# The small transposes move into the score banks: three PSUM banks plus one become four

## The chip, the cores and the metric

The kernel runs on one core of a Trainium2 chip. The metric is the device time of one execution in microseconds (us); less is better. Five engines take instructions in order, each from its own queue: TensorE (PE: matmuls and transposes; PEld is its weight load), VectorE (DVE), ScalarE (ACT), GpSimd (POOL) and SyncE (SP, which issues the DMAs).

## The reference, cut to what matters

One layer of a decoder trunk on a sequence of 2048 tokens, width 1024: an RMSNorm, one input projection, three causal attention branches (differential, forgetting, dilated), each times a SiLU gate and projected back, a sigmoid gate per channel, a sum, an output projection with residual, a last RMSNorm.

```python
h = rmsnorm(x, norm_g)
p = split(h @ w_in)                      # q, k, v, z of three branches, f, merge gates
ya = rmsnorm(diff_attention(qa, ka, va, lam, slopes)) * 0.8 * silu(za)      # 4 heads, two softmaxes each
yb = forgetting_attention(qb, kb, vb, cumsum(log_sigmoid(f + fb))) * silu(zb)  # 8 heads
yc = dilated_attention(qc, kc, vc, slopes) * silu(zc)                       # 8 heads, 3 dilations
merged = sum(sigmoid(gate_n) * (y_n @ w_branch[n]) for n in 3)
out = rmsnorm(x + merged @ w_out)
```

All of it is float32. The kernel gets near that from float16 matmuls: every operand is split into a high and a low float16 part, and a product takes three (or two) matmuls.

## The kernel before, in words

The work is cut into 12 groups, four to a branch (two heads of 64 columns each). A group has three kinds of work that are woven into each other:

- **Score work.** `softmax_rows` (L654, for the first two branches) makes, for 128 query rows, chunks of up to 512 keys. For a chunk it takes a PSUM bank with `sc_bank` (L274, pool `ps_sc`, three banks), `scores` (L641) writes two matmuls into it (L643 and L644), and one DVE operation (L678, two where the diagonal is in the chunk) adds the bias, writes the sum into an SBUF tile `e` and keeps the row maximum. With that read the bank is free. ACT then takes the exponential (L691), ACT and DVE split the tile into two float16 halves in place (L702, L703), a DMA transposes it (L712, into `eT`), which frees the `e` tile (there are five, `E_SLOTS`), and PE multiplies `eT` with the values (L695, L696) into a bank of `ps_po` (two banks). `jobs_dil` (L1007) does the same for the third branch with a bank for each block of 128 queries and two heads (DVE read at L1049, exponential at L1055).
- **Filler work.** Projections of this and the next group (`proj_unit`, `fill_v`, `fill_z`, `gate_unit`), 24 matmuls of 512 columns (L371, `mm_steps`) for each output bank of `ps_dn` (two banks).
- **Chains.** Weights are loaded a unit ahead and prepared: the largest absolute value (`abs_max`, L283), a power of two from it (`global_pow2`, L201), two splits (`w_split`, L298). `global_pow2` needs the maximum over all 128 partitions: it transposes a column on PE into a PSUM bank (L204), and DVE reduces it (L206, tile `E_...`). Before, that bank `pb_...` came from a pool of its own, `ps_tr`, with one bank. The same bank took the two prefix sums of the forgetting gates (L892 to L908, once in the kernel, by `tr_bank`, L268) and the transposed norm weights at the start (L1459). `global_pow2` is called for each weight unit, for each group's gated output (`post`, L1135), for the branch weights (`prep_b2`, L1287) and the output weights (`prep_out`, L1390): 98 calls.

So PSUM's eight banks are divided 1 (`ps_tr`) + 2 (`ps_dn`) + 3 (`ps_sc`) + 2 (`ps_po`).

Four stages follow each other in time. In the first 100 us x is normalised and transposed (`x_phase`, L623, which takes 32 turns in `ps_sc`). Then come the differential groups (to about 880 us), the forgetting groups (to about 1665 us) and the dilated groups (to about 2360 us), and last a tail with the branch projections (`branch`, L1309) and the output projection (`out_mm`, L1407). The tail takes its banks in turn from `ps_po`, `ps_sc` and `ps_dn` (`tail_bank`, L1305); the bank of `ps_tr` has no part in that.

The order of the work: `drive` (L1178) interleaves score jobs, value products and, by planned costs (`Filler.pump`, L134), filler steps and chain steps; this gives the order in which the program is written down. Beyond that the context is opened with `schedule_with_timeline_sim=True` (L1606): at build time the library takes the written order as priority, and puts each engine's instructions into an order of its own, by when, in its planned timeline, operands and a buffer of the pool are there. What engine does what when is then fixed; on the chip each engine keeps that order and waits on semaphores. The number of banks in a pool is an input to that order.

Of the kernel before, what the change touches and what calls it, by code (L numbers as in the profile page):

```python
# [11 lines left out]
F32 = mybir.dt.float32  # L12
# [4 lines left out]
PSUM = bass.MemoryType.PSUM  # L17
DRAM = bass.MemoryType.DRAM

P = 128  # L20
# [133 lines left out]
def tile_hybrid_trunk(  # L154
# [20 lines left out]
    cp = ctx.enter_context(tc.tile_pool(name="cp", bufs=1))  # L175
    st = ctx.enter_context(tc.tile_pool(name="st", bufs=4))
    dr = ctx.enter_context(tc.tile_pool(name="dr", bufs=1, space=DRAM))
    ps_tr = ctx.enter_context(tc.tile_pool(name="ps_tr", bufs=1, space=PSUM))
    ps_dn = ctx.enter_context(tc.tile_pool(name="ps_dn", bufs=2, space=PSUM))

    ident = cp.tile([P, P], F32, name="ident")
# [7 lines left out]
    def hp(n):  # L189
        return tc.high_priority(offset=n) if n else nullcontext()  # L190

    def pow2_floor(dst, src):
        V.tensor_single_scalar(dst.bitcast(I32), src.bitcast(I32), EXPMASK, op=ALU.bitwise_and)
# [5 lines left out]
        pow2_floor(dst, dst)  # L199

    def global_pow2(col, name):  # L201
        pb = ps_tr.tile([P, 512], F32, tag="tr", name=f"pb_{name}")
        with hp(H_PB):
            T.transpose(pb[:, :P], col.to_broadcast([P, P]), ident)  # L204
        E = st.tile([P, 1], F32, tag="gp", name=f"E_{name}")
        V.tensor_reduce(E, pb[:, :P], axis=AX.X, op=ALU.max)  # L206
        V.tensor_scalar(E, E, 1e-30, None, op0=ALU.max)
        pow2_floor(E, E)
        return E
# [16 lines left out]

    mn = ExitStack()
    big = mn.enter_context(tc.tile_pool(name="big", bufs=1))
    ps_sc = mn.enter_context(tc.tile_pool(name="ps_sc", bufs=3, space=PSUM))
    ps_po = mn.enter_context(tc.tile_pool(name="ps_po", bufs=2, space=PSUM))  # L230

    def e_tile(name, shape=(P, 1024), dt=F32):
# [31 lines left out]

    def gs_tile(name):
        return big.tile([P, 512], F32, tag="gs", name=name, bufs=GS)

    def tr_bank(name):  # L268
        return ps_tr.tile([P, 512], F32, tag="tr", name=name)

    def dn_bank(name):
        return ps_dn.tile([P, 512], F32, tag="dn", name=name)
# [1 line left out]
    def sc_bank(name):  # L274
        return ps_sc.tile([P, 512], F32, tag="sc", name=name)
# [41 lines left out]
    def w_scale(am, name):  # L317
        E = global_pow2(am, name)
        sw = st1("sw", f"sw_{name}", 1, 2)
        pow2_over(sw, E, 13)  # L320
        dsc = st1("dsc", f"dsc_{name}", 1, 2)
        V.tensor_scalar(dsc, E, ixs, 2.0 ** -13, op0=ALU.mult, op1=ALU.mult)
        return sw, dsc
# [509 lines left out]
    def prep_f():  # L833
        ft = bl_tile("fw")
        stg = ft[:, 0:64].rearrange("p (k c) -> p k c", c=8)
        Q.dma_start(stg, w2[:, OFF_FF:OFF_FF + 8].rearrange("(k p) c -> p k c", p=P))
        fb = st1("fb", "fb", 8, 1)
        Q.dma_start(fb, fox_fb.to_broadcast([P, 8]))
        yield 4000
        am = st1("amf", "am_f", 1, 1)  # L840
        V.tensor_reduce(am, stg, axis=AX.XY, op=ALU.max, apply_absolute_value=True)
        yield 2000
        E = global_pow2(am, "f")
        sw = st1("swf", "sw_f", 1, 1)
        pow2_over(sw, E, 13)
        wt = ft[:, 64:128].bitcast(F16).rearrange("p (a k c) -> p a k c", a=2, c=8)
        A.activation(wt[:, 0], stg, AF.Copy, scale=sw)
        V.scalar_tensor_tensor(wt[:, 1], stg, sw, wt[:, 0], op0=ALU.mult, op1=ALU.subtract)
        dsc = st1("dscf", "dsc_f", 1, 1)
        V.tensor_scalar(dsc, E, ixs, 2.0 ** -13, op0=ALU.mult, op1=ALU.mult)  # L850
        fbox.update(fb=fb, wt=wt, dsc=dsc)

    def fill_f():
# [12 lines left out]
        f = ft[:, 0:128]  # L866
# [22 lines left out]
        G.memset(one, 1.0)  # L889
        G.affine_select(out=tri, in_=one, pattern=[[1, P]], compare_op=ALU.is_ge, fill=0.0, base=0, channel_multiplier=-1)  # L890
        yield 4000
        pc = tr_bank("pcum")  # L892
        T.matmul(pc[:, 0:128], tri, f, start=True, stop=True)
        T.matmul(pc[:, 128:256], one, f, start=True, stop=True)
        tot_ = ft[:, 896:1024]
# [6 lines left out]
            V.tensor_add(tot[:, b], tot[:, b], tot[:, b - 1])  # L902
        V.tensor_add(cs[:, 1:NB], cs[:, 1:NB], tot[:, 0:NB - 1])
        yield 5000
        pt = tr_bank("pcs")
        T.transpose(pt[:, :P], cs_, ident)
        csT = ft[:, 128:256]
        A.activation(csT, pt[:, :P], AF.Copy)  # L908
# [226 lines left out]
    def post(gr):  # L1135
# [13 lines left out]
        am = yield from abs_max(z, "u" + n)  # L1149
        yield YU  # L1150
        E = global_pow2(am, "u" + n)
        s = st1("us", f"us_{n}", 1, 2)
        pow2_over(s, E, 13)
# [302 lines left out]
    xb0 = x_load(0)  # L1456
    gx = cp.tile([P, KC], F32, name="gx")
    ixs = cp.tile([P, 1], F32, name="ixs")
    pb = ps_tr.tile([P, 512], F32, tag="tr", name="pb_g")  # L1459
    T.transpose(pb[:, :KC], g8, ident[:KC, :KC])  # L1460
    V.tensor_copy(gx, pb[:, :KC])
    gm = st.tile([P, 1], F32, tag="gm", name="gm")
# [147 lines left out]
```

## Time and profile before

| | us |
|---|---|
| three timed runs | 2789.35 (median), 2782.40, 2799.62 |
| the profiled execution: first to last instruction (span) | 2783.2 |
| PE busy in it | 2624.6 (94%) |
| DVE busy | 2088.2 (75%) |
| ACT busy | 1661.3 (60%) |
| POOL busy | 376.8 (14%) |
| mean granted PE clock | 0.985 |

The profiled execution's own device time isn't given beside its span; its span lies 6.15 us under the median of the timed runs and inside their spread. "Busy" is the union of instruction times; a PE matmul's record overlaps the next one's. "Idle before" an instruction is the time in which its engine had nothing running, and the name behind the arrow is what released it. The granted clock is 1.00 at 2.4 GHz and 0.50 at 1.2 GHz.

### The profile page before, as it was taken

How to read it: one execution, taken by the hardware profiler on the slowest of the kernel's cores; microseconds unless marked ns; L12 is line 12 of the kernel's file. 1: busy time of each engine (PE TensorE's matmuls, PEld its weight loads, DVE VectorE, ACT ScalarE, POOL GpSimd, SP SyncE). 2: the span in 40 equal slices, each digit the busy share in tenths (PEclk: the TensorE clock that was granted, in tenths of full speed). 3: DMA queues.
4: the chain of work that ended last, by engine and by line, in shares of the span. 5: the costliest groups of instructions: out<-in, count | busy, mean ns of one | idle time of the engine just before them, and what ended most of it. 6: DMA issues, size and time to landing. Idle time of an engine off the chain costs nothing.

```text
span 2783.2 us, 47508 instructions
## 1 busy us (share of the span) xinstructions
PE 2624.6 (94%) x16216; PEld 1376.9 (49%) x16216; DVE 2088.2 (75%) x7048; ACT 1661.3 (60%) x3616; POOL 376.8 (14%) x529
## 2 busy tenths in 40 slices
PE   7999899999999999999899999999999999999998
PEld 4454445455444454444444444554554545444565
DVE  8687877978877878768778776658568575778955
ACT  6466666656556676666666665656657678535411
POOL 0000200200201112002102110005033051210000
PEclk9999999989999999999999999999999999999999
DMA  4345444445454786787787777648568599875232
GB/s 160 76 84 114 74 100 107 104 76 123 87 100 106 135 173 142 155 154 157 144 155 145 141 144 156 132 108 180 126 132 185 125 210 230 226 210 163 80 121 76
DMA packets 979268, 376.94 MB, mean 135 GB/s; under 512 B 834120, under 2 KB 939344, under 8 KB 977488
## 3 DMA queue, kind: packets, MB, share of 16 engines
q1 hardware_dynamic: 979024, 373.90, 61.9%
q8 instruction: 127, 2.08, 0.3%
q14 instruction: 117, 0.96, 0.1%
HBM read 118.14 MB, written 59.05 MB: 64 GB/s over the span
## 4 chain that ended last, share of the span: by engine, by line
PE 52%; DVE 19%; DMA 17%; ACT 7%; issue 4%; POOL 1%; SPq 1%; DVEq 0%; ACTq 0%; POOLq 0%
DMA eT_g<-e_g 11%; PE pg L371 10%; PE pbr L371 8%; PE pq_g L371 8%; PE pz_g L371 5%; PE pout L1417 4%; PE s_g L643 4%; DVE e_g L678 4%; PE s_g L644 4%; DVE e_g L703 4%; PE po_g L695 3%; ACT e_g L691 3%; PE pv_g L371 2%; PE pout L1418 2%; DMA w_g<-in_w_in_dram 2%
## 5 line engine op out<-in xcount | busy, mean ns | idle before, releaser
L371 PE MATMUL pg<-xT,w_g 128*128 128x512 f16 x2304 | 554.5, 382 | 0.3 <-ACT xT L638 0.3
L691 ACT ACTIVATE e_g<-e_g,nm_g,c_g 128x1024 f32<-128x1024 f32 (+7 forms) x384 | 377.6, 984 | 263.5 <-DVE nm_g L685 227.9
L643 PE MATMUL s_g<-stk_g 128*128 128x512 f16 (+3 forms) x1024 | 352.6, 352 | 50.2 <-DVE pm_g L678 45.6
L703 DVE SCALAR_TENSOR_TENSOR e_g<-e_g 128x512 f16<-128x512 f32 (+2 forms) x480 | 316.0, 670 | 80.9 <-ACT e_g L702 79.6
L371 PE MATMUL pq_g<-xT,w_q 128*128 128x512 f16 x1536 | 369.5, 387 | 5.0 <-DVE stk_g L398 4.4
L695 PE MATMUL po_g<-v_g,eT_g 128*128 128x128 f16 (+1 forms) x2232 | 306.7, 235 | 61.5 <-DMA eT_g<-e_g 56.2
L644 PE MATMUL s_g<-stk_g,q_g 128*128 128x512 f16 (+3 forms) x1024 | 351.9, 354 | 2.6 <-DMA q_g<-stk_g 2.6
L371 PEld LDWEIGHTS <-w_g 128*128 128x128 f16 x2304 | 218.9, 99 | 229.9 <-issue 5.3
L702 ACT ACTIVATE e_g<-e_g 128x512 f16<-128x512 f32 (+2 forms) x480 | 265.0, 569 | 104.4 <-DVE e_g L703 102.3
L696 PE MATMUL po_g<-v_g,eT_g 128*128 128x64 f16 (+1 forms) x2232 | 286.3, 201 | 0.0
L695 PEld LDWEIGHTS <-eT_g 128*128 128x128 f16 x2232 | 207.2, 99 | 141.7 <-DMA eT_g<-e_g 88.4
L371 PE MATMUL pz_g<-xT,w_z 128*128 128x512 f16 x1152 | 273.1, 380 | 2.5 <-DVE stk_g L398 2.4
L371 PE MATMUL pv_g<-xT,w_v 128*128 128x512 f16 x1152 | 270.3, 382 | 4.3 <-DVE vs_g L527 4.3
L1055 ACT ACTIVATE e_g<-e_g,nm_g,c_g 128x256 f32<-128x256 f32 (+1 forms) x384 | 207.8, 543 | 91.4 <-DVE nm_g L1051 90.3
L371 PE MATMUL pbr<-u,w_b 128*128 128x512 f16 x1152 | 253.5, 381 | 0.0
L678 DVE CUSTOM_DVE_ANT_0 e_g<-s_g,bias_g 128x512 f32<-128x512 f32 (+3 forms) x320 | 187.8, 605 | 59.7 <-DMA eT_g<-e_g 51.6
L696 PEld LDWEIGHTS <-eT_g 128*128 128x128 f16 x2232 | 204.5, 99 | 49.5 <-issue 5.5
L371 PEld LDWEIGHTS <-w_q 128*128 128x128 f16 x1536 | 146.5, 100 | 166.4 <-issue 13.4
L678 DVE CUSTOM_DVE_ANT_0 e_g<-s_g,R_g 128x512 f32<-128x512 f32 (+3 forms) x288 | 171.2, 596 | 62.9 <-DMA eT_g<-e_g 55.4
L1049 DVE CUSTOM_DVE_ANT_0 e_g<-s_g,bd_g 128x256 f32<-128x256 f32 (+1 forms) x384 | 122.8, 361 | 89.0 <-PE s_g L644 44.7
L371 PEld LDWEIGHTS <-w_b 128*128 128x128 f16 x1152 | 112.9, 98 | 133.5 <-issue 2.2
L644 PEld LDWEIGHTS <-q_g 128*128 128x128 f16 x1024 | 109.2, 107 | 140.6 <-issue 62.3
(471 smaller groups left out, 4174.3 us busy)
## 6 DMA issues: line engine op xcount, KB each, us to landing
gd<-gs SPq DMA_DIRECT2D x96, 256.0 KB, 2.7
gt<-gd SPq DMA_DIRECT2D x24, 1024.0 KB, 5.3
w_g<-in_w_in_dram SPq DMA_DIRECT2D x24, 512.0 KB, 4.4
ud<-y_g SPq DMA_DIRECT2D x48, 256.0 KB, 2.8
od_g<-ro_g SPq DMA_DIRECT2D x64, 132.0 KB, 1.9
xb<-in_x_dram SPq DMA_DIRECT2D x16, 512.0 KB, 5.8
q_g<-stk_g SPq DMA_DIRECT2D x128, 64.0 KB, 2.2
w_q<-in_w_in_dram SPq DMA_DIRECT2D x32, 256.0 KB, 4.1
```

What stands on the lines that cost most here:

```text
L371: T.matmul(dst, l, r, start=(i == 0), stop=(i == n - 1))
L643: T.matmul(ps, stk[:, 0, qsl], stk[:, 1, ksl], start=True, stop=False)
L644: T.matmul(ps, q2s, stk[:, 1, ksl], start=False, stop=True)
L678: V.tensor_tensor_reduce(out=et[ch // 2][:, o + a:o + a + sw], in0=ps[:, a:a + sw], in1=b, scale=1.0, scalar=-3e38, op0=ALU.add, op1=ALU.m ...
L691: A.activation(e[:, 256:256 + w], e[:, 256:256 + w], AF.Exp, bias=nm, scale=gr["c"][u], accum_out=den_of(i))
L695: T.matmul(po, eh, vv, start=first, stop=False)
L696: T.matmul(po[:, 0], el, vv[:, 0], start=False, stop=last)
L702: A.activation(h[:, :w], f, AF.Copy, scale=scale)
L703: V.scalar_tensor_tensor(h[:, w:], f, scale, h[:, :w], op0=ALU.mult, op1=ALU.subtract)
L1049: V.tensor_tensor_reduce(out=e[:, o + w * u:o + w * u + w], in0=ps[:, 256 * u:256 * u + w], in1=bt[p, u][:, 256 - w:256], scale=1.0, scala ...
L1055: A.activation(eu, eu, AF.Exp, bias=nm[:, 2 * a + u:2 * a + u + 1], scale=gr["c"][u], accum_out=sm[:, a, 2 + u:3 + u])
L1417: T.matmul(po, ah, wo[un][k], start=k == 0, stop=False)
```

## The change

The pool `ps_tr` and the helper `tr_bank` go, `ps_sc` has four banks instead of three, and the four places that took `ps_tr`'s bank take the next bank of `ps_sc`. PSUM is then divided 2 + 4 + 2. Nothing else is changed: no instruction is added, removed or resized.

```diff
@@ -175,7 +175,6 @@
     cp = ctx.enter_context(tc.tile_pool(name="cp", bufs=1))
     st = ctx.enter_context(tc.tile_pool(name="st", bufs=4))
     dr = ctx.enter_context(tc.tile_pool(name="dr", bufs=1, space=DRAM))
-    ps_tr = ctx.enter_context(tc.tile_pool(name="ps_tr", bufs=1, space=PSUM))
     ps_dn = ctx.enter_context(tc.tile_pool(name="ps_dn", bufs=2, space=PSUM))
 
     ident = cp.tile([P, P], F32, name="ident")
@@ -199,7 +198,7 @@
         pow2_floor(dst, dst)
 
     def global_pow2(col, name):
-        pb = ps_tr.tile([P, 512], F32, tag="tr", name=f"pb_{name}")
+        pb = sc_bank(f"pb_{name}")
         with hp(H_PB):
             T.transpose(pb[:, :P], col.to_broadcast([P, P]), ident)
         E = st.tile([P, 1], F32, tag="gp", name=f"E_{name}")
@@ -226,7 +225,7 @@
 
     mn = ExitStack()
     big = mn.enter_context(tc.tile_pool(name="big", bufs=1))
-    ps_sc = mn.enter_context(tc.tile_pool(name="ps_sc", bufs=3, space=PSUM))
+    ps_sc = mn.enter_context(tc.tile_pool(name="ps_sc", bufs=4, space=PSUM))
     ps_po = mn.enter_context(tc.tile_pool(name="ps_po", bufs=2, space=PSUM))
 
     def e_tile(name, shape=(P, 1024), dt=F32):
@@ -264,9 +263,6 @@
 
     def gs_tile(name):
         return big.tile([P, 512], F32, tag="gs", name=name, bufs=GS)
-
-    def tr_bank(name):
-        return ps_tr.tile([P, 512], F32, tag="tr", name=name)
 
     def dn_bank(name):
         return ps_dn.tile([P, 512], F32, tag="dn", name=name)
@@ -889,7 +885,7 @@
         G.memset(one, 1.0)
         G.affine_select(out=tri, in_=one, pattern=[[1, P]], compare_op=ALU.is_ge, fill=0.0, base=0, channel_multiplier=-1)
         yield 4000
-        pc = tr_bank("pcum")
+        pc = sc_bank("pcum")
         T.matmul(pc[:, 0:128], tri, f, start=True, stop=True)
         T.matmul(pc[:, 128:256], one, f, start=True, stop=True)
         tot_ = ft[:, 896:1024]
@@ -902,7 +898,7 @@
             V.tensor_add(tot[:, b], tot[:, b], tot[:, b - 1])
         V.tensor_add(cs[:, 1:NB], cs[:, 1:NB], tot[:, 0:NB - 1])
         yield 5000
-        pt = tr_bank("pcs")
+        pt = sc_bank("pcs")
         T.transpose(pt[:, :P], cs_, ident)
         csT = ft[:, 128:256]
         A.activation(csT, pt[:, :P], AF.Copy)
@@ -1456,7 +1452,7 @@
     xb0 = x_load(0)
     gx = cp.tile([P, KC], F32, name="gx")
     ixs = cp.tile([P, 1], F32, name="ixs")
-    pb = ps_tr.tile([P, 512], F32, tag="tr", name="pb_g")
+    pb = sc_bank("pb_g")
     T.transpose(pb[:, :KC], g8, ident[:KC, :KC])
     V.tensor_copy(gx, pb[:, :KC])
     gm = st.tile([P, 1], F32, tag="gm", name="gm")
```

## Rows read from the trace of the kernel before

**Rows 1.** The page's first part: busy us, share of the span, instructions of PE.

```profile
PE 2624.6 (94%) x16216; PEld 1376.9 (49%) x16216; DVE 2088.2 (75%) x7048; ACT 1661.3 (60%) x3616; POOL 376.8 (14%) x529
```

**Rows 2.** Busy time by stage: stretch, its length, then each engine, clock, DMA.

```profile
0.00:100.00 100.00, 84.63 (x432) 46.89 (x433) 70.57 (x257) 58.40 (x112) 4.80 (x11) 1.00 0.41 127
...
100.00:880.00 780.00, 734.28 (x4389) 379.78 (x4388) 629.26 (x2054) 475.84 (x950) 68.99 (x61) 0.98 0.47 98
880.00:1665.00 785.00, 725.50 (x5116) 378.70 (x5114) 608.83 (x2132) 516.36 (x1053) 118.44 (x186) 1.00 0.77 148
1665.00:2360.00 695.00, 668.63 (x4075) 358.08 (x4076) 469.48 (x1761) 459.23 (x1226) 151.34 (x220) 0.97 0.74 158
2360.00:2783.20 423.20, 411.60 (x2209) 213.43 (x2207) 310.01 (x848) 151.50 (x279) 33.27 (x52) 0.99 0.49 146
```

**Rows 3.** PE's waits over the span: total us, times, longest.

```profile
PE po_g L695 <- DMA eT_g<-e_g: 56.2, 55, 3.1
PE s_g L643 <- DVE pm_g L678: 45.6, 64, 3.9
...
PE s_g L643 <- DVE s_g L1049: 3.7, 6, 1.1
```

**Rows 4.** Waits in the differential stage, 100 to 880 us.

```profile
DVE e_g L678 <- DMA eT_g<-e_g: 51.6, 31, 3.9
...
PE s_g L643 <- DVE pm_g L678: 33.8, 48, 3.9
```

**Rows 5.** Waits in the forgetting stage, 880 to 1665 us.

```profile
DVE e_g L678 <- DMA eT_g<-e_g: 71.8, 44, 4.8
...
PE po_g L695 <- DMA eT_g<-e_g: 39.1, 34, 2.4
...
PE s_g L643 <- DVE pm_g L678: 11.8, 16, 1.5
```

**Rows 6.** PE in order of time around 593 us: start, us, instruction, [idle before].

```profile
588.84 0.35 PE L371 MATMUL pf<-fw,xT 128*128 128x8 f16 x8
593.11 0.58 PE L643 MATMUL s_g<-stk_g 128*128 128x512 f16 x1 [3.91 <-DVE pm_g L678]
```

**Rows 7.** DVE in order of time before 593 us.

```profile
589.38 0.77 DVE L777 TENSOR_TENSOR den_g<-den_g 128x2 f32<-128x2 f32 x1 [2.31 <-ACT e_g L691]
...
590.63 1.81 DVE L784 SCALAR_TENSOR_TENSOR e_g<-e_g,a_g,e_g 128x1024 f32<-128x1024 f32 x2
592.36 0.68 DVE L678 CUSTOM_DVE_ANT_0 e_g<-s_g,bias_g 128x512 f32<-128x512 f32 x1
...
592.97 0.68 DVE L678 CUSTOM_DVE_ANT_0 e_g<-s_g,bias_g 128x512 f32<-128x512 f32 x1
```

**Rows 8.** All first score matmuls: count, ns min/median/max, first and last start.

```profile
L643 PE MATMUL s_g<-stk_g x1024: 216/379/634, 87.8 to 2361.9; 128*128 128x512 f16 x91, 128*128 128x256 f16 x38, 128*128 128x128 f16 x36, 128*128 128x384 f16 x6
```

**Rows 9.** PE in order of time around 1621 us.

```profile
1621.38 0.38 PE L371 MATMUL pg<-xT,w_g 128*128 128x512 f16 x1
...
1621.93 1.24 PE L371 MATMUL pg<-xT,w_g 128*128 128x512 f16 x5
```

**Rows 10.** Three stretches at the lower clock (the column behind POOL is PEclk).

```profile
103.58:113.82 10.24, 6.28 (x16) 2.00 (x16) 9.83 (x46) 5.59 (x12) 0.00 (x0) 0.50 0.38 73
339.10:342.51 3.41, 3.41 (x11) 1.32 (x9) 3.32 (x15) 3.37 (x6) 0.00 (x0) 0.50 0.46 86
584.86:601.92 17.06, 13.15 (x201) 8.89 (x199) 10.41 (x28) 12.27 (x19) 1.15 (x1) 0.50 0.49 87
```

**Rows 11.** Small transposes of L204: one group, and what PE idled for.

```profile
L204 PE MATMUL pb_ug<-ident,am_ug x12: 270/273/323, 328.7 to 2451.3; 128*128 128x128 f32 x12
...
  DVE am_g L292: 8.3, 4
```

**Rows 12.** The DVE reads (L206) of those transposes.

```profile
L206 DVE TENSOR_REDUCE E_ug<-pb_ug x12: 268/284/289, 337.1 to 2454.2; 128x1 f32<-128x128 f32 x12
```

**Rows 13.** DVE's waits over the span: dilated reads for their scores.

```profile
DVE e_g L1049 <- PE s_g L644: 44.7, 49, 3.1
```

## Prediction

> **What bounds the kernel now.** I read four views in this order: the page's busy shares, the busy time by stage, PE's waits, and then the trace in order of time around the longest of them.
>
> PE is busy for 2624.6 of 2783.2 us [rows 1], so 158.6 us is all that a better order of work can win, as long as no matmul goes away; none does. By stage [rows 2] PE idles 15.4 us in the first 100 us, 45.7 in the differential stage, 59.5 in the forgetting stage, 26.4 in the dilated stage and 11.6 in the tail. The other engines have room in every stage: DVE, the next, works 629.3 of 780 us in the differential stage, 81%.
>
> What does PE wait for [rows 3]? Two causes stand out: 56.2 us before value products, for the transposing DMA into eT, and 45.6 us before score matmuls, for the DVE read that frees a score bank, with 3.7 us more of this kind in the dilated stage. So waits for score banks cost 45.6 + 3.7 = 49.3 us, and this is what the change aims at. They sit in the differential stage above all: 33.8 us there, against 11.8 in the forgetting stage, where the wait for eT is larger with 39.1 [rows 4, 5].
>
> The longest bank wait shows how they come about [rows 6, 7]. PE's last matmul before it starts at 588.84, and the next score starts at 593.11, after 3.91 us idle. DVE meanwhile waited 2.31 us for an exponential, did the sums of a row and two combining operations (1.81 us), and only then, at 592.36, read the chunk whose bank PE needed; the next chunk's read followed at 592.97. DVE was late, with three finished chunks in front of it. A fourth bank would have let PE go on at 589.2.
>
> I paired the first 640 score chunks (the first two stages; the first and last of all score matmuls are at 87.8 and 2361.9 us [rows 8]) with their DVE reads in order. A chunk holds its bank for 4.8 us in the median; all three banks are held for 639 us; 122 chunks start within 0.15 us of the end of the read three chunks back, that is, as soon as a bank is free. Against the read four chunks back none starts sooner than 0.49 us after it. So in the order that PE has now, a fourth bank would end every one of these waits.
>
> **The change part by part.** *The fourth bank, order unchanged.* All 49.3 us of PE's idle time go. This is the upper end.
>
> *The fourth bank, order remade.* The order is not the written one: filler comes in steps of six matmuls, and around 1621 us such a step is cut into one and five with value products between them [rows 9]. The order is planned from what is free when, and with four banks it puts scores earlier until four are full in the plan. Where DVE runs behind the plan, PE then waits at the fourth bank as it now does at the third. The lower end is therefore 0, or below nothing where more scores are pulled forward than DVE follows with. The row nearest to the cost is the wait total itself; I take half of it, because DVE's lateness (2 to 4 us in the example) is about as large as what one more chunk adds (one read of 0.68 us plus the 3 us or so between chunks). Term: -25 us, bounds -49 to +10.
>
> *The clock.* Three stretches of 10.24, 3.41 and 17.06 us are granted 0.50, that is 1.2 GHz [rows 10]; in or right before each I find one of the longer bank waits (the one of 3.91 us lies in the third [rows 6]). Half of their 30.7 us, 15 us, is lost. In the third many matmuls of 8 columns run as well (those of the forgetting gates), so not all of it is the wait's doing. Term: -4 us, bounds -15 to 0.
>
> *What is late next.* PE that doesn't wait for a bank comes sooner to the value products, whose eT depends on DVE, ACT and a DMA and comes no sooner. DVE itself waits 51.6 and 71.8 us for eT in the first two attention stages, because all five e tiles are in use [rows 4, 5]; a bank doesn't change that. In the differential stage, where most of the gain lies, PE loses little to eT, in the forgetting stage much. I let a third of the 25 us come back: +8 us, bounds 0 to +25.
>
> *The transposes in the pool.* 98 transposes keep their time on PE. Each now holds a score bank from its start to its DVE read: in the group shown, 328.7 to 337.4 us for the first and 2451.3 to 2454.5 for the last [rows 11, 12]. Over the 98 pairs I find 2.9 us in the median, 8.7 at most, 316 us in all, 11% of the span. So scores have four banks nine tenths of the time, and three, as now, in the rest: no loss from the count. But a transpose now has to find a bank among the scores, and what waits behind it is a weight's scale, its two splits and then a projection. Weights are loaded a unit ahead, which covers some us. PE now idles 8.3 us in four cases before transposes of the gate weights [rows 11], because the maximum is late; that is the price of a late one, 2.1 us each. I take one or two such cases: +3 us, bounds -5 (a transpose no longer waits for the read of the one before) to +50 (the third rival).
>
> *Stages where I cost it at nothing.* In the first 100 us the 32 turns of x through the score banks get a fourth bank; PE idles 15.4 us there at most [rows 2], and mostly before operands, not banks: 0, bounds -3 to +2. In the dilated stage DVE waits 44.7 us for scores [rows 13], which a score placed earlier would shorten, but PE is busy for 96% there and is the one that sets the pace: 0, bounds -8 to +5. In the tail PE is busy for 411.6 of 423.2 us [rows 2]: 0, bounds -3 to +5. The two prefix sums are six short matmuls, once: 0.
>
> Sum: -25 - 4 + 8 + 3 = -18 us. Against the profiled execution's span of 2783.2 us that is 2765. The span lies 6.15 us below the median of the timed runs, and I add this back: 2771 us.
>
> **The rivals.** *First, the whole wait goes.* All 49.3 us end, half of the 15 us of clock comes back, nothing is returned, the transposes cost 3: -54, so 2735 us. For it: in the present order no chunk would wait, and the bank waits are mostly in the stage that loses little to eT. Against it: the order is remade.
>
> *Second, the wait changes its name.* The score loop (read, exponential, split, DMA, e tile) sets the pace, PE arrives earlier and stands before eT or before the fourth bank instead. Gain 0 to 5, transposes 3: 2783 to 2791, say 2788. For it: DVE waits 123 us for eT in two stages [rows 4, 5]. Against it: DVE is at work during the waits I looked at, and has 150 us of idle time in the differential stage. That the fourth bank isn't used belongs here too; that all three banks are held for 639 us speaks against this. [...]
>
> *Third, slower.* The small transposes lose the bank that only they used. One that is placed on PE before a bank is free, or whose maximum is late, holds up everything behind it on PE, and its late scale delays the splits and the next projection. At 2.1 us each [rows 11], 24 of the 98 cost 50 us, which eats up the 21 us of the other terms and 28 more; from there this decides. At 30 the loss is 63 - 21 = 42 us: 2831 us. Against it: the chains are run ahead of need, and a bank turns over in about 5 us.
>
> **How the numbers follow.** Forecast 0.44 (its own range 2754 to 2787), first rival 0.24, second 0.20, third 0.12. A measurement here can tell about 1% from no change, that is 28 us: faster means below 2761, slower above 2817. Faster is the first rival and the low edge of the forecast (0.07): 0.31. Slower is the third rival: 0.12. Same: 0.57. The range goes from 2728, a little below the first rival, to 2812, which leaves out the third rival and a small part of the first.
>
> **What would show it right or wrong.** Right: PE's wait before L643 for DVE falls from 45.6 us to about 25; its wait for eT grows from 56 to about 64; the stretch at 1.2 GHz around 104 or 339 us is gone; the time between a transpose of L204 and its read stays near 2.9 us. The first rival would show under 10 us before L643 and no growth before eT; the second, PE's idle time of 105 us in the first two attention stages unchanged under other names; the third, PE's idle time before L204 or before L371 (for weights) several times what it is now. The forecast is wrong if PE's idle time falls by less than 5 or more than 45 us.

## The result and the profile after

The changed kernel is slower: 2862.04 us in the median of four runs (2855.62 to 2865.36) against 2790.14 us (2782.40 to 2799.62) for the kernel before. The ratio is 1.0253, with a 95% interval of 1.0228 to 1.0278: 72 us more where I forecast 18 less, and above the 2812 us at which my range ended.

The profiled execution has a span of 2861.9 us, 78.7 more than before. Its page begins like this (PE, DVE, ACT and POOL as in [rows 1]; line numbers from the middle of the kernel on are 4 lower than before):

```profile
span 2861.9 us, 47473 instructions
...
PE 2651.6 (93%) x16216; PEld 1382.1 (48%) x16216; DVE 2088.0 (73%) x7048; ACT 1661.1 (58%) x3617; POOL 376.0 (13%) x529
```

DVE, ACT and POOL work as long as before. PE issues the same 16216 matmuls, but is busy 27.0 us longer and idle 2861.9 - 2651.6 = 210.3 us instead of 158.6, that is 51.7 us longer; 27.0 + 51.7 = 78.7 us, the whole difference. Most of the longer busy time is clock: summed over the trace, PE had 1.2 GHz granted for 127.0 us in 29 stretches, before for 87.5 us in 17. In these stretches it was at work for 112.2 us, before for 70.3, and half of the 41.9 us more, 21 us, is lost by this estimate.

PE's waits (columns as in [rows 3]) show where the idle time is:

```profile
PE po_g L691 <- DMA eT_g<-e_g: 89.8, 78, 3.4
PE s_g L639 <- DVE pm_g L674: 25.4, 41, 3.8
PE pq_g L367 <- DVE stk_g L394: 15.9, 11, 3.8
```

The wait for a score bank fell from 45.6 to 25.4 us, as forecast. The wait for eT rose by far more than that, from 56.2 to 89.8 us. PE's waits before projections (all names together, summed over the trace) rose from 14.1 to 36.9 us. Of these 13.8 and 31.2 us are waits for a bank of `ps_dn`: the projection needs the bank whose last result DVE or ACT still has to read into `stk_g`, `vs_g` or `gs`. The rest after, 5.7 us, is mostly for a weight's scale or split.

DVE's waits for eT, that is for a free `e` tile, were 51.6 us in the differential stage and 71.8 in the forgetting stage [rows 4, 5]. In the same two stages of the changed kernel (100 to 908 us, 908 to 1722 us) they are

```profile
DVE e_g L674 <- DMA eT_g<-e_g: 88.3, 37, 5.0
...
DVE e_g L674 <- DMA eT_g<-e_g: 97.4, 64, 5.2
```

So the score work now comes more unevenly: it fills the five `e` tiles and stands. That PE then has less filler left when it needs eT is my reading; no row shows it.

Cut at the first score of each stage, the stages answer to those of [rows 2] (same columns):

```profile
103.50:908.60 805.10, 741.96 (x4387) 380.82 (x4386) 626.30 (x2030) 466.48 (x936) 73.27 (x61) 0.97 0.45 92
908.60:1722.00 813.40, 737.43 (x5127) 382.34 (x5124) 620.47 (x2165) 524.42 (x1064) 113.53 (x185) 0.99 0.75 145
1722.00:2428.00 706.00, 674.33 (x4102) 359.85 (x4101) 462.18 (x1744) 457.87 (x1211) 150.63 (x221) 0.97 0.74 156
2428.00:2861.00 433.00, 412.28 (x2187) 211.95 (x2185) 311.28 (x866) 154.68 (x300) 33.82 (x52) 0.98 0.49 143
```

The kernel before, cut the same way, takes 791.2, 779.4, 703.6 and 421.0 us. The first score starts 15.6 us later than before, but the third group only 0.4 us later, so that start costs nothing. From there the loss grows: 14.0 us at the fourth group, 29.6 at the first forgetting group, 63.5 at the first dilated group, 66.3 at the last score, 78.7 at the end. It is made in the two stages that alternate scores with much else, and in the tail; the dilated stage adds 2.4.

**Where it happens in the trace.** The clearest place is the first prefix sum. PE in order of time, changed kernel:

```profile
613.38 0.59 PE L639 MATMUL s_g<-stk_g 128*128 128x512 f16 x1
...
614.19 0.63 PE L639 MATMUL s_g<-stk_g 128*128 128x512 f16 x1
...
615.68 6.09 PE L367 MATMUL pg<-xT,w_g 128*128 128x512 f16 x24
...
622.93 1.67 PE L367 MATMUL pg<-xT,w_g 128*128 128x512 f16 x7
...
624.94 13.76 PE L367 MATMUL pg<-xT,w_g 128*128 128x512 f16 x63
638.53 0.38 PE L889 MATMUL pcum<-ft 128*128 128x128 f32 x2
638.75 0.39 PE L890 MATMUL pcum<-ft 128*128 128x128 f32 x2
638.98 0.38 PE L639 MATMUL s_g<-stk_g 128*128 128x512 f16 x1
...
639.41 0.38 PE L639 MATMUL s_g<-stk_g 128*128 128x512 f16 x1
...
639.84 0.38 PE L639 MATMUL s_g<-stk_g 128*128 128x512 f16 x1
```

For 638.98 - 614.19 = 24.8 us no score is started. PE isn't idle: it runs 24 + 7 + 63 = 94 projection matmuls and some value products. Then the prefix sum comes, and right behind it three scores at once. The kernel before has this in the same place:

```profile
608.71 5.99 PE L371 MATMUL pg<-xT,w_g 128*128 128x512 f16 x27
614.54 0.22 PE L643 MATMUL s_g<-stk_g 128*128 128x128 f16 x1
...
614.65 0.38 PE L643 MATMUL s_g<-stk_g 128*128 128x512 f16 x1
...
615.95 3.40 PE L371 MATMUL pg<-xT,w_g 128*128 128x512 f16 x15
619.18 0.38 PE L643 MATMUL s_g<-stk_g 128*128 128x512 f16 x1
...
620.70 0.38 PE L893 MATMUL pcum<-ft 128*128 128x128 f32 x2
...
621.30 0.22 PE L643 MATMUL s_g<-stk_g 128*128 128x128 f16 x1
```

Scores go on until 1.5 us before the prefix sum. DVE in the changed kernel tells what the scores were behind:

```profile
621.83 0.68 DVE L674 CUSTOM_DVE_ANT_0 e_g<-s_g,bias_g 128x512 f32<-128x512 f32 x1
...
633.87 0.29 DVE L882 TENSOR_TENSOR ft<-ft 128x128 f32<-128x128 f32 x1
...
639.18 0.29 DVE L892 COPY ft<-pcum 128x128 f32<-128x128 f32 x1 [5.01 <-PE pcum L890]
...
639.66 0.68 DVE L674 CUSTOM_DVE_ANT_0 e_g<-s_g,bias_g 128x512 f32<-128x512 f32 x1
```

The prefix sum's operand `f` is ready at 634.2 us, after the long chain that computes the gates. DVE read the last score that it had at 621.83 us, and every bank was free from 622.5 on. The scores waited for no bank. They stood behind a prefix sum that stood behind its operand, and when it was there, PE still had the rest of 63 planned projection matmuls in front.

**The written order.** What holds the scores back is the library's build step. I compared, in the built programs, the order in which PE first writes the tiles of a pool with the order in which the kernel's text takes them (832 score tiles, 101 of small transposes and prefix sums):

```
tiles first written out of the written order   before   after
scores among themselves                          0        0
transposes and prefix sums among themselves      0        0
both kinds together, of 933                     73        0
```

Tiles of one pool are begun in the order in which they are written down. With two pools, 73 tiles are begun after one that is written later: 20 transposes or prefix sums that scores overtook, and 53 scores that a transpose overtook. With one pool, none. From this I infer (the planner itself leaves no trace): a transpose whose maximum isn't there yet stops the planning of every score written after it, the plan puts filler in the gap, and the scores follow in a burst. By that theory, D in the expectations below, the pool's common order is the cause and the bank count matters little. The order binds the other way too: a transpose can no longer overtake scores, so its scale can come late.

### The profile page after: what moved, and what is told of

Same layout as the page of the kernel before. It is cut to its first block, busy times and chain, and to the rows that moved or that the text cites. A ratio compares the mean times of both kernels' runs of the same rounds, so it can differ in the third digit from the quotient of the medians.

```text
span 2861.9 us, 47473 instructions
## 1 busy us (share of the span) xinstructions
PE 2651.6 (93%) x16216; PEld 1382.1 (48%) x16216; DVE 2088.0 (73%) x7048; ACT 1661.1 (58%) x3617; POOL 376.0 (13%) x529
## 4 chain that ended last, share of the span: by engine, by line
PE 43%; DMA 17%; DVE 15%; ACT 4%; issue 3%; SPq 1%; POOL 0%; DVEq 0%; ACTq 0%; POOLq 0%
DMA eT_g<-e_g 12%; PE pg L367 9%; PE pq_g L367 6%; PE pbr L367 5%; PE pz_g L367 4%; PE pout L1413 4%; PE s_g L639 4%; PE s_g L640 3%; DVE e_g L699 3%; DVE e_g L674 3%; PE po_g L691 2%; PE pv_g L367 2%; PE pout L1414 2%; DMA w_g<-in_w_in_dram 1%; ACT e_g L687 1%
## 5 line engine op out<-in xcount | busy, mean ns | idle before, releaser
L367 PE MATMUL pg<-xT,w_g 128*128 128x512 f16 x2304 | 545.9, 384 | 0.3 <-ACT w_g L298 0.3
L691 PE MATMUL po_g<-v_g,eT_g 128*128 128x128 f16 (+1 forms) x2232 | 299.1, 236 | 100.4 <-DMA eT_g<-e_g 89.8
L639 PE MATMUL s_g<-stk_g 128*128 128x512 f16 (+3 forms) x1024 | 354.0, 355 | 28.9 <-DVE pm_g L674 25.4
L367 PE MATMUL pv_g<-xT,w_v 128*128 128x512 f16 x1152 | 270.2, 383 | 12.4 <-DVE vs_g L523 5.2
L692 PE MATMUL po_g<-v_g,eT_g 128*128 128x64 f16 (+1 forms) x2232 | 280.5, 202 | 0.0
L367 PE MATMUL pbr<-u,w_b 128*128 128x512 f16 x1152 | 260.4, 388 | 6.8 <-DVE ro_g L1080 4.1
L692 PEld LDWEIGHTS <-eT_g 128*128 128x128 f16 x2232 | 204.4, 99 | 46.4 <-issue 13.8
L367 PEld LDWEIGHTS <-w_v 128*128 128x128 f16 x1152 | 111.5, 99 | 137.9 <-issue 15.4
```

The costliest lines, as they stand in the source:

```text
L367: T.matmul(dst, l, r, start=(i == 0), stop=(i == n - 1))
L639: T.matmul(ps, stk[:, 0, qsl], stk[:, 1, ksl], start=True, stop=False)
L691: T.matmul(po, eh, vv, start=first, stop=False)
L692: T.matmul(po[:, 0], el, vv[:, 0], start=False, stop=last)
```

## The experiments

All ratios are to the kernel before, run on the same chip; intervals are 95%. The kernel before had medians from 2785.2 to 2792.0 us in these groups.

**Sharing apart from the fourth bank.** `share3` is the changed kernel with three banks in `ps_sc`, so one bank of PSUM is unused:

```diff
-    ps_sc = mn.enter_context(tc.tile_pool(name="ps_sc", bufs=4, space=PSUM))
+    ps_sc = mn.enter_context(tc.tile_pool(name="ps_sc", bufs=3, space=PSUM))
```

> The small transposes and prefix sums share the score pool, but the pool keeps three banks (seven of eight banks used). Theory A, the fourth score bank lets the build place scores earlier and PE then stands before eT: little change, 2785 to 2810 us, PE's wait for eT near 56 us. Theory B, the sharing is what costs, late weight scales: most of the loss is here, 2835 to 2870 us. Theory C, any replanned order scatters the time by tens of us: anything from 2760 to 2860 us, without a pattern in the waits.

Measured: 2865.43 us, ratio 1.0271 (1.0243 to 1.0300). Its PE waits:

```profile
PE po_g L691 <- DMA eT_g<-e_g: 85.5, 67, 5.9
PE s_g L639 <- DVE pm_g L674: 44.3, 63, 2.3
PE pq_g L367 <- DVE stk_g L394: 12.6, 5, 5.1
```

That is theory B's range. The whole loss is there with three banks: +75 us. The fourth bank then takes 19 us off the wait for banks (44.3 to 25.4), but only 3 us off the time; the stages in the next section show where the rest goes.

`four_dn` gives the scores their four banks alone and puts the transposes and prefix sums in the two banks of the projections:

```diff
-        pb = sc_bank(f"pb_{name}")
+        pb = dn_bank(f"pb_{name}")
...
-        pc = sc_bank("pcum")
+        pc = dn_bank("pcum")
...
-        pt = sc_bank("pcs")
+        pt = dn_bank("pcs")
...
-    pb = sc_bank("pb_g")
+    pb = dn_bank("pb_g")
```

> Four score banks, and the small transposes and prefix sums share the two banks of the projections instead. Theory A: as slow as the changed kernel, 2845 to 2880 us, scores held in PSUM for about 6.5 us in the median as there, PE's wait for eT near 90 us. Theory B: at most as slow as before, 2750 to 2800 us, since no transpose waits behind scores. Theory C: anything from 2760 to 2880 us.

Measured: 2896.85 us, 1.0386 (1.0363 to 1.0409). Worse still, and above every range that I had expected. Here 66 of the 933 score and transpose tiles are out of written order, nearly as before, but of the 390 tiles of projections, transposes and prefix sums none is (before: 30). The price is paid by whatever shares the pool, so it isn't peculiar to the score banks. With a pool of two banks more than the order may be at work.

`oneoff` is the kernel before with only the two prefix sums moved, two tiles out of 101; the transposes keep their bank:

```diff
-        pc = tr_bank("pcum")
+        pc = sc_bank("pcum")
...
-        pt = tr_bank("pcs")
+        pt = sc_bank("pcs")
```

> Only the two prefix sum tiles, used once at about 620 us, move to the score pool; it keeps three banks and the transposes keep their own. Theories A and B: the time of before within 8 us (2782 to 2798). Theory C: the order after 620 us is planned anew, so the time differs from before by more than 15 us one way or the other.

Measured: 2813.44 us, 1.0091 (1.0064 to 1.0117), 23 us above the kernel before in the same group and outside the range of theories A and B. PE in order of time:

```profile
600.52 0.63 PE L643 MATMUL s_g<-stk_g 128*128 128x512 f16 x1
...
601.65 3.19 PE L371 MATMUL pg<-xT,w_g 128*128 128x512 f16 x14
...
605.99 1.03 PE L371 MATMUL pg<-xT,w_g 128*128 128x512 f16 x4
...
607.35 11.60 PE L371 MATMUL pg<-xT,w_g 128*128 128x512 f16 x53
618.79 0.38 PE L893 MATMUL pcum<-ft 128*128 128x128 f32 x2
...
619.23 0.38 PE L643 MATMUL s_g<-stk_g 128*128 128x512 f16 x1
```

The same gap without scores, 18.7 us here, comes with these two tiles alone.

**A fourth bank from another base.** The kernel before can't be given a fourth score bank with all else kept, as that makes nine. `po1_sc3` takes one of the value products' two banks away, and `po1_sc4` gives it to the scores; transposes stay apart in both:

```diff
-    ps_po = mn.enter_context(tc.tile_pool(name="ps_po", bufs=2, space=PSUM))
+    ps_po = mn.enter_context(tc.tile_pool(name="ps_po", bufs=1, space=PSUM))
```

> One bank instead of two for the value products, three score banks, the transposes have their own: the base for the next run. Between 2800 and 2900 us; no theory says more.

> As the run before it, with a fourth score bank and the transposes still apart. Theory A: 20 to 70 us slower than it. Theory D: not slower than it by more than 10 us, up to 40 us faster. Theory C: within 50 us either way.

Measured: 2948.02 us, 1.0573 (1.0540 to 1.0607), and 2965.30 us, 1.0632 (1.0609 to 1.0654). The base is slower than I had expected. From it the fourth bank costs 17 us, more than the 10 that theory D allows and less than the 20 that theory A asks for: PE's wait for score banks falls from 78.7 to 63.3 us, its waits for eT and behind `stk_g` rise from 44.1 to 53.3 and from 20.8 to 28.9. No gain from a fourth bank shows here, but 17 us is little more than another order makes by chance (below), and the base is another kernel.

**When the late steps are written.** `after_late2` raises planned costs in the chains, so that transposes and prefix sums are written down later, behind more scores; `before_late2` makes the same edit in the kernel before:

```diff
-YA = 3000
+YA = 9000
...
-        yield 2000
+        yield 8000
...
-        yield 4000
+        yield 10000
...
-        yield 5000
+        yield 11000
```

> The changed kernel, but the chains wait longer before they write a small transpose or prefix sum (planned 9000 instead of 3000 before the weight scales, 8000, 10000 and 11000 instead of 2000, 4000 and 5000 for the forgetting gates; the group outputs' scales as they were). Theory D, tiles of one pool are taken in the written order, so scores stand behind a transpose whose maximum isn't there yet: written later the transpose finds its operand ready, and half of the loss or more goes, 2785 to 2825 us. Theory A, the fourth bank makes scores come in bursts: still 2840 to 2880 us. Theory C, each new order scatters the time: anything from 2780 to 2880 us.

> The kernel before with the same later transposes, as the control: there they have their own bank, so theories A and D expect 2780 to 2805 us; theory C anything from 2780 to 2860 us.

Measured: 2841.00 us, 1.0172 (1.0153 to 1.0192), and 2815.21 us, 1.0083 (1.0064 to 1.0101). The edit wins 21 us in the changed kernel and costs 23 in the one before. Both miss theory D's ranges: it expected half of the loss or more to go, and the control to stay under 2805. The first lies just inside theory A's range. In the shared pool the wait for eT falls from 89.8 to 68.6 us. So the place in the text may matter to the shared pool, in the direction of theory D, but tuning it doesn't bring the loss back.

**How much any other order costs.** An order found anew may differ by chance. `jit1` and `jit2` change a planned cost slightly in the kernel before (YD from 3000 to 3050, and XF from 1.1 to 1.101); `after_jit1` and `after_jit2` do this in the changed kernel:

```diff
-YD = 3000
+YD = 3050
```

> The kernel before with one planned cost of the weight chains set from 3000 to 3050, which means nothing by itself but gives another order. Theories A and D: within 10 us of before. Theory C: 15 to 60 us away from it, and then likely slower.

> The kernel before with the planned filler stretched by 0.1% (XF 1.101 instead of 1.1), again nothing but another order. Theories A and D: within 10 us of before. Theory C: 15 to 60 us away from it, and then likely slower.

> The changed kernel with the planned cost of the weight chains at 3050 instead of 3000: another order, nothing else. If the loss of 72 us belongs to the change: 2840 to 2885 us. If it is the accident of one order: anything from 2780 to 2880, and likely under 2840.

> The changed kernel with the planned filler stretched by 0.1%: another order, nothing else. If the loss of 72 us belongs to the change: 2840 to 2885 us. If it is the accident of one order: anything from 2780 to 2880, and likely under 2840.

Measured: 1.0053 (1.0034 to 1.0072) and 1.0018 (1.0005 to 1.0030) for the kernel before, 2805.42 and 2795.56 us; 1.0271 (1.0238 to 1.0303) and 1.0263 (1.0233 to 1.0294) for the changed one, 2866.16 and 2864.83 us. The 13 us of `jit1` are more than the 10 that theories A and D allowed. Order by chance is worth up to half a per cent in these two tries, not two and a half, and the changed kernel keeps its loss in three orders. The loss belongs to the change. By the same measure `oneoff` is 0.4 to 0.7% above these two, with an interval that overlaps that of `jit1`, and `before_late2` little above `jit1`.

**The order alone.** `coupled` leaves the pools of the kernel before as they are, four pools and three score banks, and only makes PE begin score tiles, turns of x, transposes and prefix sums in their written order, by a dependency that orders the issue without a wait on the chip:

```diff
+    turn = [None]
+
+    def in_turn(ins):
+        if turn[0] is not None:
+            tc.add_manual_dep(ins.ins, turn[0].name, mybir.DependencyInfo(mybir.DependencyClass.NoSync, mybir.DependencyReason.DATA), reason="in_turn")
+        turn[0] = ins.ins
...
-            T.transpose(pb[:, :P], col.to_broadcast([P, P]), ident)
+            in_turn(T.transpose(pb[:, :P], col.to_broadcast([P, P]), ident))
```

and so for the first matmul of each other tile of the kinds named. `coupled_ug` orders only the scores, the turns of x and the 12 transposes for the groups' output scales (`pb_u...`); `coupled_rest` orders all but these 12.

> The kernel before with its own four pools and banks, but PE has to start the small transposes, prefix sums, transposes of x and scores in the order in which they are written (an order of issue, no wait for a result). Theory D, the loss of the change is this order, which a shared pool imposes: 2840 to 2880 us, though not one bank is shared. Theory A or a loss from the shared bank itself: within 20 us of before, 2780 to 2810. Theory C, any other order: 2790 to 2815, as the runs with slightly changed planned costs.

> As the run before it, but only the 12 transposes for the scale of a group's output are bound to the scores' order. Theory D with these as the ones written long before their operand is there: 2815 to 2850 us, half of the loss or more from an eighth of the transposes. If the transposes for the weights carry the loss: under 2812 us.

> The complement: all but those 12 are bound to the scores' order. Theory D with the 12 as the main cause: 2795 to 2825 us. If the transposes for the weights and the prefix sums carry the loss: 2830 to 2870 us.

Measured: `coupled` 2835.92 us, 1.0160 (1.0143 to 1.0177); `coupled_ug` 2808.78 us, 1.0065 (1.0050 to 1.0080); `coupled_rest` 2831.98 us, 1.0149 (1.0128 to 1.0170). No tile is moved, and about 45 us are lost: 4 us less than the low end of theory D's range, and well above those of A and C. `coupled_ug` and `coupled_rest` both came out as expected if the transposes for the weights and the prefix sums carry the loss. PE in `coupled`, at one of the 12 transposes:

```profile
749.82 0.38 PE L652 MATMUL s_g<-stk_g 128*128 128x512 f16 x1
...
752.64 4.05 PE L378 MATMUL pq_g<-xT,w_q 128*128 128x512 f16 x18
758.30 0.28 PE L706 MATMUL po_g<-v_g,eT_g 128*128 128x256 f16 x1 [1.61 <-DMA eT_g<-e_g]
...
759.60 0.28 PE L211 MATMUL pb_ug<-ident,am_ug 128*128 128x128 f32 x1
759.72 0.33 PE L652 MATMUL s_g<-stk_g 128*128 128x384 f16 x1
...
760.04 0.38 PE L652 MATMUL s_g<-stk_g 128*128 128x512 f16 x1
...
760.48 0.38 PE L652 MATMUL s_g<-stk_g 128*128 128x512 f16 x1
```

The picture is that of the shared pool: scores stop, filler runs, the transpose comes, scores follow in a burst. I counted the gaps of more than 8 us between starts of scores from 100 us on: 31 before, 34 and 33 in `jit1` and `jit2`, 47 in `coupled`, 45 after. Of these gaps 1 ends within 1 us behind a small transpose or prefix sum before, 1 and 0 in `jit1` and `jit2`, and 9 each in `coupled` and after: so many can be put down to them one by one. The 12 output scales carry little (`coupled_ug` is near `jit1`), although the gap shown is at one of them; the weights' transposes and the prefix sums carry nearly all. PE's waits in `coupled`:

```profile
PE po_g L706 <- DMA eT_g<-e_g: 63.5, 60, 5.0
PE s_g L652 <- DVE pm_g L689: 43.3, 64, 2.4
PE pq_g L378 <- DVE stk_g L405: 15.6, 6, 5.4
```

PE's waits before projections are nearly as long as in the changed kernel (15.6 us in the last row, 32.5 under all names; 14.1 before); the wait for eT has grown by 7.3 us only. DVE's wait for a free `e` tile has grown at once: over the span 153.8 us before, 166.5 and 156.5 in `jit1` and `jit2`, 201.4 in `coupled`, 202.7 in `share3`, 224.9 after.

The order also holds back the transposes. From the last write to a transpose's operand to its start it takes 3.2 us in the median before, 3.2 and 2.9 in `jit1` and `jit2`, 6.7 in `coupled`, 11.8 in `share3`, 5.7 after. No run separates what late transposes cost from what scores behind transposes cost. `coupled_jit1` and `share3_jit1` repeat the two steps with YD at 3050:

> The run coupled with the planned cost of the weight chains at 3050 instead of 3000. If the 45 us of that run belong to the order between transposes and scores: 2825 to 2855 us. If they are one order's accident: under 2815 or over 2865.

> The run share3 with the planned cost of the weight chains at 3050 instead of 3000. If the shared pool with three banks is as slow as the changed kernel by itself, so that the fourth bank gives back next to nothing: 2845 to 2885 us. If share3 was slow by accident and the fourth bank is worth something: clearly off, under 2840 or over 2890.

Measured: 2838.82 us, 1.0184 (1.0167 to 1.0201), and 2868.33 us, 1.0295 (1.0279 to 1.0310), both in the range expected. The times hold under another order; the waits don't. PE's wait for eT is 61.5 us in `jit1`, 73.0 in `coupled_jit1` and 91.5 in `after_jit1`, but in `share3_jit1`

```profile
PE po_g L691 <- DMA eT_g<-e_g: 69.0, 53, 6.1
```

**Without transposes on PE.** `three_dma` and `four_dma` replace each small transpose by two DMAs over DRAM, so that three and four score banks compare with nothing in the pool but scores and turns of x:

```diff
-        with hp(H_PB):
-            T.transpose(pb[:, :P], col.to_broadcast([P, P]), ident)
+        gxd = dr.tile([P, 1], F32, tag="gxd", name=f"gxd_{name}", bufs=4)
+        Q.dma_start(gxd, col)
+        pb = st.tile([P, P], F32, tag="gxb", name=f"pb_{name}", bufs=1)
+        Q.dma_start(pb, gxd.rearrange("p o -> (o p)").unsqueeze(0).to_broadcast([P, P]))
```

> No small transposes on PE at all: the 98 maxima over partitions go to DRAM and back as a row for every partition by two DMAs on SP's queue, three score banks, the two prefix sums in the projections' banks. The base for the next run, and free of the order between transposes and scores. Two small DMAs take longer than a transpose (2 to 6 us against about 3), so weight scales come later: 2785 to 2840 us.

> As the run before it, with a fourth score bank: the bank alone, with no transpose among the scores. If the fourth bank is worth what the prediction took (half of the 49 us of bank waits, a third of it given back): 10 to 30 us faster than the run before it. If it is worth nothing by itself, since the order then places scores earlier and PE waits for eT instead: within 10 us of it. If it makes scores come in bursts that harm: 10 to 40 us slower.

Measured: 3471.83 us, 1.2430 (1.2388 to 1.2472), and 3464.99 us, 1.2414 (1.2378 to 1.2451): no difference between three and four. But the base, far above the 2840 us that I expected at most, is another kernel. In `three_dma` SP's queue stands between the two DMAs, and all other DMAs behind it:

```profile
SPq L204 <- DMA gxd_g<-am_g: 131.7, 21, 9.4
```

So this says nothing certain about the fourth bank in the kernel in question.

## Why the prediction was wrong

The steps from one kernel to the other, in medians and ratios to the kernel before:

| step | us | ratio | with YD at 3050 |
|---|---|---|---|
| before | 2790 | 1 | 2805, 1.0053 (`jit1`) |
| written order among scores and transposes, pools untouched (`coupled`) | 2836 | 1.0160 | 2839, 1.0184 |
| one pool of three banks (`share3`) | 2865 | 1.0271 | 2868, 1.0295 |
| a fourth bank in it (the change) | 2862 | 1.0253 | 2866, 1.0271 |

The order by itself costs 46 and 33 us, the shared pool 29 more in both. The fourth bank's -3 and -2 us lie inside the intervals.

**The step that failed is "The transposes in the pool"**, +3 us with bounds of -5 and +50. It measured 75 us, before to `share3` (63 with YD at 3050), of which 46 (33) come with the order alone. I argued that there was "no loss from the count", as a transpose holds a bank for 2.9 us, 11% of the span, and that "a transpose now has to find a bank among the scores". The hold was right: 2.7 us in the median after, 291 us in all. But I left out the reverse direction: scores now have to take their turn behind transposes as well. I costed occupation of banks, and at least half of the cost is one of order. That a pool hands out its banks in written order could have been asked of the kernel before: scores and transposes each keep their own order in it, but not a common one.

**The two prefix sums, costed at 0,** belong to the same mistake. They are short matmuls (five in the trace, not six), but the first waits for the long chain of the gates. Moved alone (`oneoff`) they come with 0.9%, 0.4 to 0.7% above orders changed by chance; since the intervals of `oneoff` and `jit1` overlap, a price of their own isn't shown.

**"The fourth bank, order remade",** -25 us, of which the next term let 8 come back, measured -3 (2865.43 to 2862.04). The sum hides a gain and a loss. `share3` in the differential stage and in the tail (columns as above):

```profile
104.80:926.50 821.70, 751.31 (x4417) 384.29 (x4415) 629.58 (x2048) 472.99 (x945) 73.07 (x61) 0.97 0.45 93
...
2440.60:2861.20 420.60, 406.75 (x2178) 210.63 (x2176) 308.29 (x848) 151.20 (x283) 33.98 (x51) 0.99 0.49 146
```

All stages, in us, from first score to first score, the tail from the last score to the end:

| stage | `share3` | the change | `share3_jit1` | `after_jit1` |
|---|---|---|---|---|
| differential | 822 | 805 | 826 | 809 |
| forgetting | 817 | 813 | 817 | 815 |
| dilated | 697 | 706 | 696 | 711 |
| tail | 421 | 434 | 421 | 434 |

The fourth bank wins 17 us in the differential stage and loses 13 in the tail, in both orders. `jit1` and `jit2` move these two stages by at most 8 and 5 us; they move the other two by up to 20, so what the table shows there may be chance. So in the shared pool the two terms' 17 us were about won, in the stage where I placed most of the gain, and largely lost again where I had costed nothing.

But the row that I priced isn't what made the gain, so it is luck that the size agrees. In the differential stage PE's wait for score banks is 19.8 us in `share3` and 19.7 after; in the forgetting stage it falls from 24.5 to 5.7, and the stage by 4. Over the span it fell from 45.6 to 25.4 us where I expected 25; in `after_jit1` and `after_jit2` it is 33.3 and 31.8, so the near hit is partly luck. The 8 us that I let come back before eT are 33.6 us in the changed kernel. In the order shown 29.3 of them are there in `share3`, with YD at 3050 only 7.5 above `jit1`, so they can't be given to one step.

The Trainium skill, "TensorE: Matmul & The Clock Gate", section "HAM oscillation", tells of a matmul kernel with its loop reordered that had no further gain from PSUM double-buffering (126.6 and 125.5 us). The 3 us here are as little, but the stages show a gain and a loss in them. The Trainium skill's "Perfetto Trace Analysis", section "Matmul Optimizations", says to see that all eight PSUM banks are used; `share3` uses seven and is 3 us slower than the change, so in the sum the eighth bank hardly counts here.

**The clock,** -4 us, went the other way: 21 us lost by the estimate above. The stretches at 104 and 339 us are gone as I said, but in all there are 29 instead of 17. One stretch of the changed kernel (columns as in [rows 10]):

```profile
596.71:617.19 20.48, 16.63 (x294) 11.73 (x291) 14.66 (x41) 14.50 (x23) 1.33 (x1) 0.50 0.30 58
```

It answers to the one at 584.86 in [rows 10], 17.06 us long. More idle time goes with more of them. I take the clock for a consequence; no run shows it apart.

**The stages at nothing.** The first 100 us were right in the end (0.4 us late at the third group), the dilated stage too (+2.4, inside -8 to +5). The tail was not: +12.3 us with bounds of -3 and +5, and 12.7 and 13.2 in `after_jit1` and `after_jit2`. The transposes for the branch and output weights, which take turns there with the tail's own banks, aren't enough for it: with them in a pool of three banks the tail is 0.8 us shorter than before, in both orders. The loss comes with the fourth bank. PE idles 13.2 us in that tail and 6.2 in `share3`'s, and has 1.2 GHz for 19.2 us against 7.3; what in the order does it, no run shows.

**The rivals.** The second was right that the wait changes its name to eT, but put it at no loss (by its own terms its range is 2787 to 2792 us, not 2783 to 2791). The third had the right sign, and the right place, transposes that come late. Its first mechanism, PE standing before a transpose, was wrong. The 8.3 us in four cases that I took from [rows 11] hold the idle time of the weight load too; PE alone idles 3.7 us in two cases there. What PE alone idles before these transposes is 12.4 us before and 10.0 after. The row of `am_g` before, and the two largest after:

```profile
PE pb_g L204 <- DVE am_g L292: 3.7, 2, 3.6
...
PE pb_ug L203 <- DVE am_o L288: 4.0, 1, 4.0
...
PE pb_ug L203 <- DVE am_ug L288: 2.2, 2, 1.1
```

The item of `am_g` is down to 0.2. Its second mechanism, a late scale that holds up the next projection, shows with 5.7 us at most in PE's waits; what the plan has hidden of it shows in no row. In the gap at 614 us the plan has filled the lateness with projections, so no wait shows at the place where the loss is made. Where it shows later depends on the order: before eT in the changed kernel; in `share3_jit1`, against `jit1`, with 7.5 us more before eT and 58.8 us more at 1.2 GHz (141.7 and 82.9).

My sign of being wrong was met: PE's idle time, which was to fall, rose by 51.7 us.

**What stays open.** The 29 us between `coupled` and `share3` are measured twice (2836 to 2865, 2839 to 2868), but not explained. They arise in the differential stage (799 to 822 us, 799 to 826) and the forgetting stage (801 to 817, 809 to 817); the dilated stage gives 15 back. The number of long gaps between scores doesn't grow (47 and 41), and the wait for eT grows in one order (63.5 to 85.5 us) but not in the other (73.0 to 69.0). What does grow in both is the lateness of the transposes, to 11.8 us in the median from 6.7 and 7.1, and the fourth bank takes it back to 5.7 and 6.7, together with about half of the loss in the differential stage. That late scales are the cause is only argued: in `before_late2` the transposes start 10.9 us late in the median, and its differential stage is no longer than before. The value of a fourth bank to the kernel before, transposes apart, couldn't be tried with eight banks. None of the kernels tried is faster than the kernel before.

## What to carry to other kernels

Before two kinds of work share a buffer pool, ask in what order the pool is handed out, not only how long each holds a buffer: a short, rare user that waits for a long chain can hold back a frequent one that is ready, and the other way round. A bank of its own for such a user can be worth more than another bank for the bottleneck's longest wait. And where instructions are placed by a planner, look for the loss not at a wait but at gaps between starts of the critical work that are filled with something else, and measure first what a neutral change of order is worth. Before you call a buffer worthless, compare stage by stage: -17 and +13 us stood behind the -3.

## What the hardware showed that I had not expected

A wait of PE is not the price of the buffer that it waits for. From `share3` to the change the wait for score banks fell by 18.8 us in the forgetting stage and the stage by 4; in the differential stage the wait stayed where it was and the stage fell by 17. And with a round trip of two small DMAs on the queue that issues the others the kernel took 24% longer: in the row above the queue stands until the first of the two has landed, up to 9.4 us at a time.
